# Attention: remainders of the weights of heads 1 to 7 and of the output product by ScalarE and an accumulating transfer

## The chip, the cores and the metric

The kernel runs on one core of a Trainium2 chip. The metric is device time in microseconds (us) of one execution. The core has five instruction streams that run side by side and meet at semaphores: TensorE (PE, the matmuls, with PEld for its weight loads), VectorE (DVE), ScalarE (ACT), GpSimd (POOL) and SyncE (SP). DMA transfers are issued from a queue of SP (the loads of the weights) or of POOL.

## The reference, cut to what matters

The program is a two-layer decoder: one state-space layer with a gated FFN, then one attention layer with a gated FFN, on 512 tokens of width 1024. The change lies in the attention layer, which has 8 heads and a causal mask:

```python
c_q = rms_norm(h @ q_down, q_norm_g)
q = (c_q @ q_up).reshape(b, s, 8, 128 + 64)
k_nope = (c_kv @ kv_up_k).reshape(b, s, 8, 128)
...
scores = (einsum('bqhd,bkhd->bhqk', qn, k_nope)
          + einsum('bqhr,bkr->bhqk', qr, k_rope)) * scale
p = softmax(where(key_idx <= q_idx, scores, -inf))
o = einsum('bhqk,bkhd->bqhd', p, v)
mix = o.reshape(b, s, 1024) @ out_proj
h = layer_norm(DN_ALPHA * h + mix)
```

## The kernel before, in words

**Weights.** Each fp32 product runs as three passes of a rounded format. A weight tile s is split into h, which is s rounded, and the remainder l = s - h; the activations are split alike, and the matmuls compute h·x0 + l·x0 + h·x1 (`mm_a` at lines 159, `mm_b` at lines 165 to 167: h with x0, l with x0, h with x1). `WStream` feeds the weights in a fixed order. `load` issues a tile's transfer on SP into one of six staging buffers `wst` (at most three of them loaded and not yet split), `_split` takes the next tile, writes h into a `wh` buffer on ScalarE (line 96) and l into a `wl` buffer on VectorE (line 97), and lets `fill` issue the next load. There are six `wh` and six `wl` buffers. A buffer can be written again when PE has read the tile that was in it for the last time, so tile i+6 is split only after tile i is done with. `ahead` splits tiles before they are wanted, `get` hands one out, `retire` marks one as read.

**Attention.** `mla_items` lists the tiles: those of the down projections and of v, then `hw[h]` for h = 0 to 7 (128 x 640, the weights of q and k of head h), then `ow[0..7]` (128 x 1024, the rows of the output product that belong to a head). After the down projections, the rotary part `qr` (its last addition is on POOL, line 1119) and v, the program runs a loop over the heads. Iteration h has, in the program's order: `qk(h+1)` and, for even h+1, `qk_rope(h+1)`; the split of one tile; `pv(h-1)`, which sums the head's output in one PSUM bank and splits it into `oT` (ScalarE line 1307, VectorE line 1308); `ptrans(h)`, which transposes the softmax numbers `E` on PE and splits them into `PT` (lines 1290 and 1291); `scores(h+1)`, four query blocks of 128, 256, 384 and 512 keys, with a mask, a maximum, an exponential and a division per block. An iteration with `qk_rope` is called a rope iteration below. The output product comes in two parts: `out_piece(0, 2, i)` uses ow0 and ow1 with heads 0 and 1, `out_piece(2, 6, i)` uses ow2 to ow7. So ow6 and ow7 go into the buffers that ow0 and ow1 leave.

**Order.** The instructions on SP stand in the order of the code. Those of the other engines are put in order by a scheduler when the program is built, so a change in the code can move instructions that it doesn't touch. On the chip each engine takes its instructions strictly in that order.

Of the kernel before, what the change touches and what calls it, by code (L numbers as in the profile page):

```python
# [13 lines left out]
AF = mybir.ActivationFunctionType  # L14
ALU = mybir.AluOpType
# [3 lines left out]
P = 128  # L19
# [9 lines left out]


class WStream:

# [41 lines left out]
    def _split(self, nst=None):  # L76
        nc = self.k.nc
        i = self.split
        f, kind, part = (self.items[i][1:] + (None, None))[:3]
        if kind == "=":  # L80
            self.st[i] = self.st["+"]
        elif i not in self.st:
            self.load(i)
        s = self.st.pop(i)
        if kind == "+":
            self.st["+"] = s
            r = self.sums[part]
            nc.vector.tensor_tensor(r[:, :f], r[:, :f], s[:, :f], op=ALU.add)  # L88
            s = r
        elif kind == "-":  # L90
            nc.vector.tensor_tensor(s[:, :f], self.sums[part][:, :f], s[:, :f], op=ALU.subtract)
        if kind not in ("r", "a", "+"):
            self.out -= 1
        h = self.k.wh.tile([P, 1024], F32R, name="wh")
        l = self.k.wl.tile([P, 1024], F32R, name="wl")
        nc.scalar.copy(h[:, :f], s[:, :f])  # L96
        nc.vector.tensor_tensor(l[:, :f], s[:, :f], h[:, :f], op=ALU.subtract)  # L97
        self.w[i] = (h, l)
        self.split += 1
        self.fill(nst)  # L100
# [956 lines left out]
AH, QR, KVR, RD = 8, 384, 256, 64  # L1057
# [7 lines left out]
def mla_items(dw, vw, rw, hw, ow):  # L1065

    it = [(dw[j], 1024) for j in range(4)] + [(dw[j][:, :768], 768) for j in (4, 5)]
    rv = rw.rearrange("(k p) n -> p k n", p=P)
    it += [(rv[:, 0:2, :], 1024), (rv[:, 2:3, :], 512)]
    vv = vw.rearrange("(k p) n -> p k n", p=P)  # L1070
    it += [(vv[:, :, hf * 512:(hf + 1) * 512], 1024) for hf in range(2)]
    it += [(hw[h], 640) for h in range(AH)]
    it += [(ow[j * P:(j + 1) * P, :], 1024) for j in range(AH)]
    return it


# [318 lines left out]
def trunk_kernel(tc, *aps):  # L1395
    d = dict(zip(_INS, aps))
    out = aps[len(_INS)]
    with ExitStack() as ctx:
        ctx.enter_context(tc.manual_schedule(engines={mybir.EngineType.SP}))
        k = K(tc, ctx)  # L1400
        items = ssd_items(d['xbc'], d['zdt'], d['zw'], d['sow'])
        items += ffn_items(d['up'][0], d['down'][0], RP0)
        items += mla_items(d['dw'], d['vw'], d['rw'], d['hw'], d['aow'])
        items += ffn_items(d['up'][1], d['down'][1], RP1)
        ws = WStream(k, items, k.nb, 3, k.la)
        n = ssd(k, ws, 0, d['xT'], d['x'], d['cw4'], d['hv'], d['sng'], d['gb'][0])
        n = ffn(k, ws, n, d['cw3'][0], d['gb'][1], RP0, la=5, mid=lambda: rope_tables(k, d['pos'], d['freq']))
        n = mla(k, ws, n, d['ang'], d['gb'][2])
        n = ffn(k, ws, n, d['cw3'][1], d['gb'][3], RP1, out=out)
# [53 lines left out]
```

## Time and profile before

| | before |
|---|---|
| median of 3 runs | 1312.31 us (1311.85 to 1312.35) |
| profiled execution | 1311.7 us, of which the span of the profile 1310.0 us |
| PE busy | 1299.5 us, 99% of the span |
| DVE busy | 1020.6 us, 78% |
| ACT busy | 636.0 us, 49% |
| POOL busy | 93.1 us, 7% |
| chain that ended last | PE 95%, DVE 4%, ACT 1% |

The busy times are sums over the span. The chain is followed back from the last instruction, at each step to what released it. The profiled execution is 0.6 us under the median of the runs. TensorE's granted clock was full in the whole span.

### The profile page before, as it was taken

Reading aid. Unit: us, or ns where it says so; the run is one execution under the profiler, and the core shown is the slowest. Engines: PE = TensorE matmul, PEld = TensorE weight load, DVE = VectorE, ACT = ScalarE, POOL = GpSimd, SP = SyncE. Lnnn points to the kernel's source line nnn. Section 1 sums busy time; section 2 is a strip of 40 time slices with the busy share of each in tenths; the row PEclk is TensorE's granted clock in tenths of the full one; section 3 lists DMA queues with packets and bytes.
Section 4 is the critical chain, followed back from the end, with each engine's and each line's share of the span. In section 5 each row is a group of like instructions: output and inputs, shape, how many; then the busy total and the mean of one; then the engine's idle time right before and its main releaser. Section 6 shows DMA issues by size and latency. Waiting matters only on the chain.

```text
span 1310.0 us, 17422 instructions
## 1 busy us (share of the span) xinstructions
PE 1299.5 (99%) x6666; PEld 1098.9 (84%) x6666; DVE 1020.6 (78%) x1581; ACT 636.0 (49%) x1029; POOL 93.1 (7%) x96
## 2 busy tenths in 40 slices
PE   9999999999999999999999999999999999999997
PEld 8888888888888988888888899888898888888886
DVE  7888888797798868866766876898587686667587
ACT  6765555455453544444443434665254444444341
POOL 0111011011011001100000012000100010000000
PEclk9999999999999999999999999999999999999999
DMA  8423322313410433352311822121144227323251
GB/s 297 179 113 129 113 88 90 132 58 133 161 65 10 171 129 81 80 207 98 123 58 31 254 81 62 71 107 49 35 149 135 79 35 213 130 97 105 41 161 65
DMA packets 49779, 144.59 MB, mean 110 GB/s; under 512 B 5312, under 2 KB 6336, under 8 KB 48416
## 3 DMA queue, kind: packets, MB, share of 16 engines
q1 hardware_dynamic: 44480, 133.57, 28.8%
q0 software_dynamic: 5072, 9.77, 4.4%
q8 instruction: 52, 0.85, 0.3%
q14 instruction: 31, 0.25, 0.1%
q10 hardware_dynamic: 144, 0.15, 0.0%
HBM read 141.30 MB, written 2.16 MB: 110 GB/s over the span
## 4 chain that ended last, share of the span: by engine, by line
PE 95%; DVE 4%; ACT 1%; issue 0%; DVEq 0%; ACTq 0%
PE ps L159 57%; PE ps L165 10%; PE ps L167 10%; PE ps L166 10%; PE ps L803 1%; PE ps L915 1%; PE ps L811 1%; PE ps L274 1%; PE ps L792 1%; PE ps L742 1%; PE ps L1265 1%; DVE wl L97 1%; DVE PT L1291 1%; PE ps L770 1%; DVE E L1279 0%; DVE smx L1275 0%
## 5 line engine op out<-in xcount | busy, mean ns | idle before, releaser
L159 PE MATMUL ps<-ht,wh 128*128 128x512 f32 (+1 forms) x2256 | 517.0, 379 | 0.0
L159 PEld LDWEIGHTS ps<-ht,wh 128*128 128x128 f32 x2256 | 408.1, 188 | 79.7 <-issue 1.4
L97 DVE TENSOR_TENSOR wl<-wst,wh 128x1024 fp32r<-128x1024 f32 (+3 forms) x222 | 256.3, 1169 | 44.2 <-ACT wh L96 43.3
L96 ACT CAST wh<-wst 128x1024 fp32r<-128x1024 f32 (+3 forms) x222 | 218.8, 995 | 114.3 <-PE ps L167 62.3
L159 PE MATMUL ps<-ht,wl 128*128 128x512 f32 (+1 forms) x1128 | 266.6, 378 | 0.0
L159 PEld LDWEIGHTS ps<-ht,wl 128*128 128x128 f32 x1128 | 205.2, 188 | 39.6
L328 DVE SCALAR_TENSOR_TENSOR acc<-ps,cw,acc 128x511 f32<-128x511 f32 x88 | 65.7, 747 | 80.0 <-ACT acc L327 80.0
L165 PE MATMUL ps<-wh,gt 128*128 128x512 f32 (+1 forms) x320 | 123.7, 387 | 0.0
L167 PE MATMUL ps<-wh,gt 128*128 128x512 f32 (+1 forms) x320 | 123.6, 386 | 0.0
L166 PE MATMUL ps<-wl,gt 128*128 128x512 f32 (+1 forms) x320 | 123.6, 386 | 0.0
L340 ACT CAST gt<-acc 128x512 fp32r<-128x512 f32 (+1 forms) x80 | 44.0, 571 | 102.0 <-DVE acc L333 99.3
L657 DVE SCALAR_TENSOR_TENSOR cv<-ps,cw,cv 128x511 f32<-128x511 f32 (+2 forms) x96 | 71.3, 746 | 26.8 <-ACT cv L655 25.9
L327 ACT ACTIVATE acc<-ps,cw 128x512 f32<-128x512 f32 x88 | 68.3, 776 | 29.5 <-PE ps L159 29.4
L167 PEld LDWEIGHTS ps<-wh,gt 128*128 128x128 f32 x320 | 60.1, 188 | 12.3
L332 ACT ACTIVATE acc<-acc 128x512 f32<-128x512 f32 x44 | 27.8, 632 | 87.6 <-DVE acc L329 87.5
L165 PEld LDWEIGHTS ps<-wh,gt 128*128 128x128 f32 x320 | 60.1, 188 | 12.1
L166 PEld LDWEIGHTS ps<-wl,gt 128*128 128x128 f32 x320 | 60.1, 188 | 12.1
L329 DVE SCALAR_TENSOR_TENSOR acc<-ps,cw,acc 128x510 f32<-128x510 f32 x88 | 65.8, 748 | 2.5
L52 POOL DMA_DIRECT2D rs<-in_down_dram x24 | 25.4, 1058 | 572.7 <-DVE wl L97 572.7
L96 ACT CAST wh<-rs 128x1024 fp32r<-128x1024 f32 (+1 forms) x48 | 39.9, 834 | 46.4 <-DVE rs L88 27.1
L341 DVE TENSOR_TENSOR gt<-acc,gt 128x512 fp32r<-128x512 f32 (+1 forms) x80 | 48.8, 627 | 13.5 <-ACT gt L340 13.5
L387 DVE SCALAR_TENSOR_TENSOR h<-h,ps 128x512 f32<-128x512 f32 x56 | 37.6, 686 | 26.0 <-PE ps L167 26.0
(242 smaller groups left out, 1744.7 us busy)
## 6 DMA issues: line engine op xcount, KB each, us to landing
wst<-in_up_dram SPq DMA_DIRECT2D x88, 512.0 KB, 3.5
wst<-in_xbc_dram SPq DMA_DIRECT2D x32, 512.0 KB, 6.0
wst<-in_down_dram SPq DMA_DIRECT2D x26, 512.0 KB, 5.5
W<-cumd SPq DMA_DIRECT2D x8, 1024.0 KB, 4.6
wst<-in_sow_dram SPq DMA_DIRECT2D x16, 512.0 KB, 3.6
wst<-in_zw_dram SPq DMA_DIRECT2D x14, 512.0 KB, 6.1
rs<-in_down_dram POOLq DMA_DIRECT2D x12, 512.0 KB, 6.9
wst<-in_down_dram SPq DMA_DIRECT2D x18, 256.0 KB, 2.6
```

Source lines behind the costliest of these rows:

```text
L96: nc.scalar.copy(h[:, :f], s[:, :f])
L97: nc.vector.tensor_tensor(l[:, :f], s[:, :f], h[:, :f], op=ALU.subtract)
L159: nc.tensor.matmul(out, w[:, k, :], xts[k][:, x, ts], start=first and p == 0 and k == 0, stop=last and p == 2 and k == nk - 1, skip_group_ ...
L165: nc.tensor.matmul(out, xt[:, 0, tsl], wh, start=start, stop=False, skip_group_check=True)
L166: nc.tensor.matmul(out, xt[:, 0, tsl], wl, start=False, stop=False, skip_group_check=True)
L167: nc.tensor.matmul(out, xt[:, 1, tsl], wh, start=False, stop=stop, skip_group_check=True)
L327: nc.scalar.activation(a, b, AF.Identity, bias=cw[:, ch, 3:4], scale=cw[:, ch, 2:3])
L328: nc.vector.scalar_tensor_tensor(a[:, 1:], b[:, :SEQ - 1], cw[:, ch, 1:2], a[:, 1:], op0=ALU.mult, op1=ALU.add)
L329: nc.vector.scalar_tensor_tensor(a[:, 2:], b[:, :SEQ - 2], cw[:, ch, 0:1], a[:, 2:], op0=ALU.mult, op1=ALU.add)
L340: k.nc.scalar.copy(dst[:, 0, :], src)
L341: k.nc.vector.tensor_tensor(dst[:, 1, :], src, dst[:, 0, :], op=ALU.subtract)
L657: nc.vector.scalar_tensor_tensor(t[:, d:], b[:, :SEQ - d], cw[:, ch, 3 - d:4 - d], t[:, d:], op0=ALU.mult, op1=ALU.add)
```

## The change

The remainder of 15 of the 16 tiles that the head loop and the output product use, `hw[1]` to `hw[7]` and `ow[0]` to `ow[7]`, is made in another way. They carry the kind "d". ScalarE writes minus the rounded tile into `wl`, and a transfer issued by GpSimd adds the staged tile to it, so that `wl` holds s - h as before. The VectorE subtraction is left out for these tiles. In the changed kernel line 96 is line 97, the new lines are 99 and 100, and lines after `_split` have numbers higher by 5.

```diff
         nc.scalar.copy(h[:, :f], s[:, :f])
-        nc.vector.tensor_tensor(l[:, :f], s[:, :f], h[:, :f], op=ALU.subtract)
+        if kind == "d":
+            nc.scalar.activation(l[:, :f], s[:, :f], AF.Copy, scale=-1.0)
+            nc.gpsimd.dma_start(l[:, :f], s[:, :f], accum_op=ALU.add)
+        else:
+            nc.vector.tensor_tensor(l[:, :f], s[:, :f], h[:, :f], op=ALU.subtract)
...
-    it += [(hw[h], 640) for h in range(AH)]
-    it += [(ow[j * P:(j + 1) * P, :], 1024) for j in range(AH)]
+    it += [(hw[h], 640) + ("d",) * (h > 0) for h in range(AH)]
+    it += [(ow[j * P:(j + 1) * P, :], 1024, "d") for j in range(AH)]
```

On VectorE 15 subtractions go; on ScalarE 15 operations of the same tile sizes come, on GpSimd 15 DMA issues, seven of 128 x 640 and eight of 128 x 1024 fp32. The first place is ScalarE in iteration h=3, a rope iteration, from `qk_rope(4)` to the first `PT`. Before:

```order
L1251 ACTIVATE qrT_7709<-ps 64x512
L1251 ACTIVATE qrT_7712<-ps 64x512
L96 CAST wh<-wst 128x1024
L1307 CAST oT<-ps 128x512
L1290 CAST PT_7742<-ps 128x512
L1290 CAST PT_7749<-ps 128x384
```

And now:

```order
L1256 ACTIVATE qrT_7717<-ps 64x512
L1256 ACTIVATE qrT_7720<-ps 64x512
L97 CAST wh<-wst 128x1024
L99 ACTIVATE wl<-wst 128x1024
L1312 CAST oT<-ps 128x512
L1295 CAST PT_7751<-ps 128x512
```

The new operation stands between the rounding of the weight tile and `oT`, and the same holds in each iteration from h=2 to h=6. The second place is ScalarE at the end of the loop, from the last `PT` of head 7 to the first square sum of the layer norm, where ow6 and ow7 are split. Before:

```order
L1290 CAST PT_8253<-ps 128x256
L1290 CAST PT_8258<-ps 128x128
L96 CAST wh<-wst 128x1024 x2
L1307 CAST oT<-ps 128x512
L194 ACTIVATE lnjunk,lnst<-h,lnst 128x1024
```

And now:

```order
L1295 CAST PT_8271<-ps 128x128
L99 ACTIVATE wl<-wst 128x1024
L97 CAST wh<-wst 128x1024 x2
L99 ACTIVATE wl<-wst 128x1024
L1312 CAST oT<-ps 128x512
L199 ACTIVATE lnjunk,lnst<-h,lnst 128x1024
```

Minus the rounded ow6 now comes first, that of ow7 after both roundings and before `oT`. The third place is PE in `out_piece(2, 6, 0)`, where the first PSUM bank (`ps_8338` before, `ps_8353` now) takes its last three products, those with ow7 (`wh_8332`, `wl_8333` before, `wh_8346`, `wl_8347` now). Before:

```order
L165 MATMUL ps_8338<-wh_8332,oT_8328 128x512
L166 MATMUL ps_8338<-wl_8333,oT_8328 128x512
L167 MATMUL ps_8338<-wh_8332,oT_8328 128x512
L165 MATMUL ps_8339<-wh_7838,oT_7734 128x512
L166 MATMUL ps_8339<-wl_7839,oT_7734 128x512
L167 MATMUL ps_8339<-wh_7838,oT_7734 128x512
```

And now:

```order
L170 MATMUL ps_8353<-wh_8346,oT_8342 128x512
L170 MATMUL ps_8354<-wh_7847,oT_7743 128x512
L171 MATMUL ps_8354<-wl_7848,oT_7743 128x512
L172 MATMUL ps_8354<-wh_7847,oT_7743 128x512
L170 MATMUL ps_8354<-wh_7982,oT_7867 128x512
L171 MATMUL ps_8353<-wl_8347,oT_8342 128x512
L172 MATMUL ps_8353<-wh_8346,oT_8342 128x512
```

Four matmuls of the second bank (`ps_8354`) now stand ahead of the first one that reads the remainder of ow7.

## Rows read from the trace of the kernel before

**Rows 1.** The page: busy us, share of the span, instructions of each engine.

```profile
PE 1299.5 (99%) x6666; PEld 1098.9 (84%) x6666; DVE 1020.6 (78%) x1581; ACT 636.0 (49%) x1029; POOL 93.1 (7%) x96
```

**Rows 2.** Stretches: busy us of each engine, summed over 830 to 920 us.

```profile
sum 90.00, PE 88.12 PEld 76.90 DVE 81.72 ACT 54.79 POOL 0.00; mean PE 9.79 PEld 8.54 DVE 9.08 ACT 6.09 POOL 0.00
```

**Rows 3.** Waits of PE, whole span: engine, line, releaser, us, times, longest.

```profile
PE ps L1288 <- DVE E L1279: 1.0, 2, 0.7
PE ps L1265 <- DVE oT L1308: 0.8, 3, 0.3
PE ps L1265 <- DVE kT L1236: 0.2, 1, 0.2
```

**Rows 4.** Timeline of PE, iteration h=3: start us, us, instruction, idle before.

```profile
869.78 0.34 PE L1265 MATMUL ps<-kb,qrT 128*128 128x384 f32 x1
870.37 0.96 PE L1265 MATMUL ps<-kT,qT 128*128 128x512 f32 x3 [0.25 <-DVE oT L1308]
```

**Rows 5.** Chain of waits, iterations h=1 to h=2: start us, us, what.

```profile
851.14 0.73 DVE wl L97
```

**Rows 6.** Chain of waits, iteration h=3.

```profile
868.37 1.23 DVE wl L97
...
869.62 0.70 DVE oT L1308
```

**Rows 7.** Chain of waits, iteration h=4.

```profile
878.58 0.60 DVE oT L1308
```

**Rows 8.** Chain of waits, iterations h=6 and h=7.

```profile
899.92 0.60 DVE oT L1308
...
902.80 0.47 ACT E L1277 x2
...
907.35 0.88 PE ps L1288 x6
```

**Rows 9.** Timeline of ACT, iterations h=4 and h=6.

```profile
876.27 1.04 ACT L96 CAST wh<-wst 128x1024 fp32r<-128x1024 f32 x1
...
896.48 1.99 ACT L96 CAST wh<-wst 128x1024 fp32r<-128x1024 f32 x2
...
898.84 1.43 ACT L1290 CAST PT<-ps 128x512 fp32r<-128x512 f32 x4
```

**Rows 10.** Groups by form, 780 to 925 us: busy us, mean ns, idle before.

```profile
L97 DVE TENSOR_TENSOR wl<-wst,wh 128x1024 fp32r<-128x1024 f32 x11 | 13.3, 1222 | 0.7 <-ACT wh L96 0.7
L97 DVE TENSOR_TENSOR wl<-wst,wh 128x640 fp32r<-128x640 f32 x8 | 7.6, 956 | 0.0
```

**Rows 11.** Timeline of the tail, PE and ACT.

```profile
915.14 0.39 PE L166 MATMUL ps<-wl,oT 128*128 128x512 f32 x1
...
915.79 2.00 ACT L96 CAST wh<-wst 128x1024 fp32r<-128x1024 f32 x2 [6.60 <-PE ps L167]
...
921.14 0.39 PE L166 MATMUL ps<-wl,oT 128*128 128x512 f32 x1
...
921.82 0.39 PE L166 MATMUL ps<-wl,oT 128*128 128x512 f32 x1
```

**Rows 12.** DMA of 513 to 521 us: issues, KB each, median us to landing.

```profile
rs<-in_down_dram POOLq DMA_DIRECT2D x1, 512.0 KB, 5.6
rs<-in_down_dram POOLq DMA_DIRECT2D x1, 256.0 KB, 4.1
```

**Rows 13.** Line 52, the accumulating loads on POOL, whole span.

```profile
L52 POOL DMA_DIRECT2D rs<-in_down_dram x24: 860/1056/1407, 507.0 to 1258.0; - x24
...
DMA to landing us min/median/max: 4.0/6.7/9.8
```

**Rows 14.** DMA of 780 to 925 us, SP's loads of ow.

```profile
wst<-in_aow_dram SPq DMA_DIRECT2D x8, 512.0 KB, 3.5
```

**Rows 15.** Timeline of POOL and PE ahead of the head loop.

```profile
823.04 1.80 POOL L1119 TENSOR_TENSOR qr<-qr,rtmp 128x512 f32<-128x512 f32 x1 [5.52 <-DVE qr L1118]
...
824.74 0.60 PE L1247 MATMUL ps<-ident,qr 128*128 128x128 f32 x4
```

## The prediction

> **What bounds the kernel now.** The busy shares come first: PE is busy in 99% of the span, VectorE in 78%, ScalarE in 49%, GpSimd in 7% [rows 1]. So VectorE's work is worth something only where PE waits for it. The waits of PE name such places: 2.0 us in all (1.0 + 0.8 + 0.2) in six waits, for the last division of a softmax, for `oT` and for `kT` [rows 3], all of them in the head loop. There VectorE is nearly full, 81.7 of 90 us, while ScalarE has 35 us to spare [rows 2]. A wait row understates the loss, because it is counted from the modelled end of the matmul before. The starts show it: between 869.78 and 870.37 lie 0.59 us [rows 4], where a matmul of 128x384 needs 0.17 (three of 128x512 take 0.68 us from 921.14 to 921.82 [rows 11], 0.23 each, and three quarters of that). The loss is 0.42 and the wait row says 0.25, so I add 0.17 to 0.18 to each of six waits: 2.0 + 6 x 0.18 = 3.1 us. That is all that an unburdened VectorE can give back, 0.24% of the time.
>
> The chain of waits says how those stalls arise. From iteration h=1 to 907.35 us it runs on VectorE and ScalarE alone, and PE only catches up with it; it ends with PE's transposes of head 7 [rows 8]. So what decides there is the length of this chain, from one `oT` to the next, and no sum of busy times.
>
> **What goes and what comes.** VectorE loses eight subtractions of 1.21 us (13.3 / 11) and seven of 0.95 (7.6 / 8) [rows 10], about 16 us. ScalarE gets fifteen operations instead, and I price them as the rounding of the same tile: 2.00 us for two of 128x1024 in a row, 1.99 in another place [rows 9, 11], less the overlap, so 0.95 each. Below that they can hardly come, the shape being the same; a lone one may take 1.04 [rows 9]. GpSimd gets fifteen DMA issues of about 1.1 us each [rows 13], on an engine that does little else. Only the seats on the chain count, so I walk along it.
>
> **The head loop, iteration by iteration.**
> - h=1 to h=2: the subtraction on the chain at 851.14 (0.73 us) goes [rows 5], and the maxima, exponentials and the division for which PE waited up to 0.7 us [rows 3] come that much earlier. ScalarE has its idle gap after `PT` for the new operation. -0.75.
> - h=3 (rope): now the subtraction begins at 868.37, when the weight is rounded, and `oT` at 869.62 [rows 6]. After the change the new operation takes 0.95 on ScalarE from there (869.3), `oT`'s rounding 0.5, a hop 0.05: `oT` on VectorE begins at about 869.87. +0.25. VectorE is free, but it is late because ScalarE now does in a row what the two did side by side.
> - h=4: rounding begins at 876.27 [rows 9], ends 0.95 later, then 0.95 and 0.5: 878.7, against 878.58 [rows 7]. +0.1.
> - h=5 (rope): as h=3. +0.25.
> - h=6: before, two tiles were rounded together from 896.48 [rows 9] and subtracted together, and `oT` began at 899.92 [rows 8]. Now one is split first: 896.48 + 0.95 + 0.95 + 0.5 = 898.9, a gain of 1.0. But then ScalarE does `PT` (1.43 us [rows 9]) and the second tile (1.9) ahead of the exponentials: 898.95 + 1.43 + 1.9 = 902.3, against 902.80 [rows 8]. -0.45, and it lasts to 907.35.
>
> Sum -0.6. The bounds: -3.1, if every stall goes, and +0.6, if only the three losses come. I take -0.6, since it follows the order of the changed ScalarE.
>
> **The tail.** Here ow6 and ow7 are split, into buffers that `out_piece(0, 2, 3)` leaves late, and now a transfer stands between the split and PE. PE reads the remainder of ow0 last at 915.14 + 0.39 [rows 11]. ScalarE writes minus the rounded ow6 from 915.55 to about 916.6 (1.04 for a lone one), and GpSimd issues the transfer. Then come both roundings (1.9, to 918.5) and minus the rounded ow7 (to 919.45), and GpSimd issues at 919.48. PE wants the remainder of ow6 at 921.14. That of ow7 it wanted at 921.82 [rows 11]; the four matmuls that were moved ahead make it 921.82 + 4 x 0.23 = 922.73. With a landing L after the issue the first stall is 916.6 + L - 921.14, and both together are 919.48 + L - 922.73 = L - 3.25, if L is over 3.3. VectorE had both remainders ready at about 919.4, before PE asked, so this is a loss from zero. Nothing hides it: PE has taken all that it could take ahead, and its order is fixed.
>
> L is the uncertain price. No transfer within SBUF stands in the trace. The nearest are the FFN's accumulating loads on the same queue: 5.6 us for 512 KB and 4.1 for 256 KB when little else moves [rows 12], a median of 6.7 and up to 9.8 over all [rows 13]. A plain load of ow on SP, 512 KB in rows of 4096 bytes, takes 3.5 [rows 14]. The new transfer has 512 KB in 128 rows of 4096 bytes, as many rows as the 256 KB one with rows of 2048 bytes, so 4.1 is the bound below. I take 5.6, by the row with the same bytes and the same addition on the way. The tail costs 5.6 - 3.25 = +2.35; with 4.1 it is +0.85, with 6.7 +3.45.
>
> The Trainium skill, page "DMA: Bandwidth & Descriptors", section "Anatomy of one DMA — SWDGE (gpsimd) path", fits such a transfer as 2.0 us plus the bytes over 436 GB/s, which gives an estimate of 3.2 us for 512 KB. The plain load's 3.5 is near it, the accumulating load's 5.6 is not [rows 12, 14], so I let the measurement decide.
>
> **What is hidden.** In h=1 to h=5 the tiles are split some 10 us and more before PE reads them (one tile an iteration, up to six ahead), and their transfers land within that even at 9.8 us. The staging buffer is now freed by the landing, some 6 us later, and SP's loads behind it wait; with six buffers and at most three unsplit, a spare one is there. The FFN's first tiles wait there too, but they are read only after the layer norm. The transfers of heads 1 and 2 stand on GpSimd among the `qr` additions. The last addition ran from 823.04 for 1.80 us, and PE transposes its result at 824.74 [rows 15], a tie. An issue of 1.1 us in front of it begins when ScalarE has written `wl`, near 821.5, and ends about 822.6, so it is hidden by 0.4 us; without that cover it costs up to 0.7.
>
> **Sum.** -0.6 + 2.35 = +1.75 us. The profiled span becomes 1311.75 and its execution, with 1.7 us around the span, 1313.45. The median of the runs lies 0.6 over the profiled execution: 1312.31 + 1.75 = 1314.06, so **1314.1 us**.
>
> **The rivals.**
> - *The transfer of the tail is slow* (slower). The loads of the FFN's weights start just then, and beside other traffic an accumulating transfer took 6.7 us in the median and 9.8 at most [rows 13]. Then the tail costs 3.45 to 6.55 and the time is 1315.2 to 1318.3 us. It decides from L = 6.45 on, where the sum passes 2.6 us, which is 0.2% and about what a measurement can tell from no change. For it: ow6's landing frees a staging buffer and so starts a load that runs beside ow7's transfer. Against it: one load of 512 KB takes 3.5 us and there are at most two. 0.3, and 0.06 more for a chain that loses at every iteration (+0.6) beside an L of 5.6, 1315.3 us.
> - *The transfer is short* (no change). If the new transfer costs no more than a plain load, whose 3.5 us is close to the 3.3 from which a wait begins, the tail loses at most 0.25 us and the head loop's -0.6 stays: 1311.7 to 1312.0 us. For it speaks that the rows are the plain load's 4096 bytes [rows 14], against it every accumulating row. 0.08. The Trainium skill's rule of 3.2 us (the page named above) would end here.
> - *VectorE's relief is the whole story* (faster). The chain of the head loop becomes shorter than PE's work, every stall goes: -3.1. With a tail that costs nothing, 1309.2 us; it decides if the tail costs under 0.5, L under 3.75. For it speaks VectorE's 91% in the loop, against it that `oT` waits for ScalarE, which gets longer. 0.06.
>
> **How the numbers follow.** The forecast has the remaining 0.5, and lies between +0.2 (L of 4.1) and +2.6, so 1312.5 to 1314.9 by itself. Within 0.2% are forecast and short transfer, 0.58; slower 0.36; faster 0.06. The range leaves out the fastest case and the slowest third of the slow transfer: 1311.3 to 1316.8 us.
>
> **What the changed profile would show.** In the waits of PE a new line 171 (the product with l) that waits for a DMA, twice, with some 1.1 and 1.3 us, and the wait for E of up to 0.7 us gone. In the landing times of line 100, medians near 5.6 for 512 KB. `oT` of the rope iterations still on the chain, with ScalarE's line 99 ahead of it in place of VectorE's subtraction. VectorE's busy time lower by about 16 us, and the FFN of the same length. I am wrong if line 99 takes much more than 0.95 us, if PE waits for line 99's `wl` in the loop, or if the transfer slows VectorE or the loads beside it.

## The result, and the profile after

| | before | after |
|---|---|---|
| median of 12 runs each | 1312.28 us (1311.85 to 1312.97) | 1315.41 us (1314.97 to 1315.73) |
| ratio after to before | | 1.0023, interval 1.0015 to 1.0031 |
| profiled execution, its span | 1311.7, 1310.0 us | 1315.5, 1313.5 us |

The change costs 3.1 us (by the interval of the ratio 2.0 to 4.1). The first row of the page shows what was meant to happen to the busy times, against [rows 1]:

```profile
PE 1300.5 (99%) x6666; PEld 1098.5 (84%) x6666; DVE 1005.4 (77%) x1566; ACT 647.7 (49%) x1044; POOL 105.5 (8%) x111
```

VectorE does 15 us less, ScalarE 12 us more, and PE's work is the same. The waits of PE (engine, line, releaser: us, times, longest) are to be held against [rows 3]:

```profile
PE ps L1270 <- DVE oT L1313: 1.8, 2, 1.0
PE ps L171 <- DMA wl<-wst: 1.7, 1, 1.7
...
PE ps L1270 <- DVE kT L1241: 0.2, 1, 0.2
```

The waits for E are too short to be listed now, those for `oT` have doubled, and one for the new transfer is there. The two traces have the same 6666 matmuls, so I compared the start of the same matmul in both (us; the last column is what the stretch since the row above added):

```
place                              before   after   later by   added
second product, early              10.43    10.92    +0.49     +0.49
h=2, first transpose after E      857.29   857.28    -0.01     -0.50
h=3, first matmul after oT        870.37   871.00    +0.63     +0.64
h=4, transpose that needs E       877.25   878.16    +0.91     +0.28
h=5, first matmul after oT        890.58   892.09    +1.51     +0.60
h=6, transpose that needs E       897.45   899.16    +1.71     +0.20
h=6, first matmul after oT        900.58   902.02    +1.44     -0.27
h=7, transpose that needs E       907.35   908.46    +1.11     -0.33
tail, after ow7                   923.18   926.61    +3.43     +2.32
```

The first 0.49 us are no effect of the change: in the thirteen profiles of this study other than that of before this point came 0.0 to 1.2 us later than there, whatever the kernel. Up to the end of the head loop the change loses 0.62 us, in the tail 2.32, 2.94 together. The -0.50 of head 2 is the sum of a new wait for `oT` in h=1, +0.22, and of the wait for E, which is gone, -0.72. Outside these rows the two kernels keep step within 0.15 us, the whole second FFN too.

What happened in a rope iteration, VectorE's timeline shows (h=3; start us, us, instruction, idle before it), to be read beside [rows 6]:

```profile
866.40 0.68 DVE L1257 SCALAR_TENSOR_TENSOR qrT<-ps,qrT 64x512 fp32r<-64x512 f32 x1
867.75 0.69 DVE L1257 SCALAR_TENSOR_TENSOR qrT<-ps,qrT 64x512 fp32r<-64x512 f32 x1 [0.66 <-ACT qrT L1256]
870.25 0.69 DVE L1313 TENSOR_TENSOR oT<-ps,oT 128x512 fp32r<-128x512 f32 x1 [1.81 <-ACT oT L1312]
```

VectorE, freed of the subtraction, stands idle for 1.81 us and waits for ScalarE. ScalarE's timeline has the reason:

```profile
867.12 0.59 ACT L1256 ACTIVATE qrT<-ps 64x512 fp32r<-64x512 f32 x1 [1.12 <-DVE qrT L1257]
867.62 1.03 ACT L97 CAST wh<-wst 128x1024 fp32r<-128x1024 f32 x1
868.55 1.06 ACT L99 ACTIVATE wl<-wst 128x1024 fp32r<-128x1024 f32 x1
869.63 0.59 ACT L1312 CAST oT<-ps 128x512 fp32r<-128x512 f32 x1
```

Rounding and minus the rounded tile stand in a row ahead of `oT`, for which PE waits. In h=2 VectorE waits in the same way, though PE does not (VectorE's timelines, before and now):

```profile
858.28 0.68 DVE L1308 TENSOR_TENSOR oT<-ps,oT 128x512 fp32r<-128x512 f32 x1
```

```profile
858.59 0.69 DVE L1313 TENSOR_TENSOR oT<-ps,oT 128x512 fp32r<-128x512 f32 x1 [1.45 <-ACT oT L1312]
```

In the tail, GpSimd's timeline has the two issues and PE's timeline the two waits, beside [rows 11]:

```profile
917.96 0.86 POOL L100 DMA_DIRECT2D wl<-wst  x1 [12.95 <-ACT wl L99]
920.95 0.86 POOL L100 DMA_DIRECT2D wl<-wst  x1 [2.13 <-ACT wl L99]
```

```profile
921.95 0.39 PE L170 MATMUL ps<-wh,oT 128*128 128x512 f32 x1
922.43 0.50 PE L171 MATMUL ps<-wl,oT 128*128 128x512 f32 x1
...
923.92 0.39 PE L170 MATMUL ps<-wh,oT 128*128 128x512 f32 x1
926.03 0.50 PE L171 MATMUL ps<-wl,oT 128*128 128x512 f32 x1 [1.73 <-DMA wl<-wst]
```

ow6's remainder comes 0.25 us late (0.48 where 0.23 is the pace), ow7's 1.88 (2.11), and a little is lost at the start after each. And the transfers of 919 to 927 us (issues, KB each, median us to landing):

```profile
wst<-in_up_dram SPq DMA_DIRECT2D x2, 512.0 KB, 4.8
wl<-wst POOLq DMA_DIRECT2D x1, 512.0 KB, 5.0
```

### The profile page after: what moved, and what is told of

Same layout as the page of the kernel before. It is cut to its first block, busy times and chain, and to the rows that moved or that the text cites. A ratio compares the mean times of both kernels' runs of the same rounds, so it can differ in the third digit from the quotient of the medians.

```text
span 1313.5 us, 17451 instructions
## 1 busy us (share of the span) xinstructions
PE 1300.5 (99%) x6666; PEld 1098.5 (84%) x6666; DVE 1005.4 (77%) x1566; ACT 647.7 (49%) x1044; POOL 105.5 (8%) x111
## 4 chain that ended last, share of the span: by engine, by line
PE 97%; DVE 1%; DMA 1%; ACT 1%; issue 0%; SPq 0%; DVEq 0%; ACTq 0%
PE ps L164 58%; PE ps L171 10%; PE ps L170 10%; PE ps L172 10%; PE ps L1270 1%; PE ps L808 1%; PE ps L816 1%; PE ps L1307 1%; PE ps L279 1%; PE ps L797 1%; PE ps L747 1%; PE ps L1293 1%; PE ps L920 1%; PE ps L775 1%; DMA xst<-in_xT_dram 0%; DMA wl<-wst 0%
## 5 line engine op out<-in xcount | busy, mean ns | idle before, releaser
L102 DVE TENSOR_TENSOR wl<-wst,wh 128x1024 fp32r<-128x1024 f32 (+3 forms) x207 | 239.9, 1173 | 43.1 <-ACT wh L97 40.6
```

## The experiments

The theory after the result: the change loses at two places, in the head loop because ScalarE makes `oT` later, and in the tail because the last two transfers land late. Each experiment ran against the kernel before on the same chip; its ratio has its interval.

### Which tiles lose: heads only, all but the last two, the last two only

The edits, each to the changed kernel:

```diff
 heads only:
-    it += [(ow[j * P:(j + 1) * P, :], 1024, "d") for j in range(AH)]
+    it += [(ow[j * P:(j + 1) * P, :], 1024) for j in range(AH)]
 last two subtracted (on VectorE, as before):
+    it += [(ow[j * P:(j + 1) * P, :], 1024) + ("d",) * (j < 6) for j in range(AH)]
 last two only:
+    it += [(hw[h], 640) for h in range(AH)]
+    it += [(ow[j * P:(j + 1) * P, :], 1024) + ("d",) * (j >= 6) for j in range(AH)]
```

> Only the weights of heads 1 to 7 take the new way, all eight tiles of the output product are split as before. Theory (the change loses at two places, where ScalarE makes minus the rounded tile of ow ahead of oT, and in the tail where the transfers of ow6 and ow7 land after PE asks): neither place has the new work, so no loss is left, and the wait of PE for E in head 2, 0.7 us and more before, goes: 1311.4 to 1312.3 us, -0.8 to 0 against before. Rival (the transfers or the issues on GpSimd slow the other engines or the loads, or the 0.5 us by which the profiled execution of the changed kernel was later from its 10th microsecond on belongs to the change): 1312.8 us or more, +0.5.

> The changed kernel, but ow6 and ow7 are split on ScalarE and VectorE as before. Theory: the tail's loss goes whole, and the loss of the head loop stays: 1312.6 to 1313.4 us, +0.3 to +1.1 against before; PE waits for no transfer. Rival (the tail's loss is oT of head 7 behind a longer ScalarE, or the transfers crowd the FFN's loads): over 1314.3 us.

> The kernel before, but ow6 and ow7 take the new way. Theory: the tail's loss alone, +2.1 to +2.4 us, 1314.4 to 1314.7 us, with a wait of PE for the transfer of over 1.5 us and landings of 4.5 to 5.1 us; the head loop as before. Rival (the loss comes from the sum of all new transfers): under +1 us, 1313.3 us or less.

Measured: heads only 1311.99 us, ratio 0.9998 (0.9989 to 1.0007); last two subtracted 1312.67 us, 1.0003 (0.9994 to 1.0012); last two only 1314.51 us, 1.0016 (1.0007 to 1.0025). All three lie in the ranges that were forecast for them. So the last two tiles carry 2.1 of the 3.1 us. With heads only, PE's matmuls come 0.50 us earlier from head 2 on, and 0.39 of it is left at the end of the loop; the median's gain of 0.4 us is inside its interval. PE's waits where the last two tiles alone take the new way:

```profile
PE ps L171 <- DMA wl<-wst: 1.4, 2, 1.2
...
PE ps L1293 <- DVE E L1284: 0.9, 2, 0.6
PE ps L1270 <- DVE oT L1313: 0.7, 3, 0.3
```

and where all but they do:

```profile
PE ps L1270 <- DVE oT L1313: 1.8, 2, 0.9
```

The first list is that of before [rows 3] with the transfer added. The second has the two long waits for `oT` and no other one of the loop left. By its trace that kernel loses 0.61 us in the loop; the runs' 0.3 us cannot be told from no change.

### ScalarE's order: the split after oT, with and without the change

```diff
-                with tc.issue_after(a.ins), tc.issue_after(d.ins):
-                    ws.ahead(n[0], most=1)
 ...
-                pv(h - 1)
+                a, d = pv(h - 1)
+            if h + 1 < AH:
+                with tc.issue_after(a.ins), tc.issue_after(d.ins):
+                    ws.ahead(n[0], most=1)
```

(`pv` returns the two instructions that write `oT`.) The same edit was made to the changed kernel, to the kernel before, and to the changed kernel with ow6 and ow7 subtracted on VectorE.

> The changed kernel, but in the loop the split of a weight tile is asked for after oT, so that ScalarE makes oT first and then rounds the tile and writes minus the rounded tile. Theory: the waits of PE for oT in iterations h=3 and h=5 (about 1.1 and 1.0 us) vanish or shrink to under 0.3 each, the tail stays at +2.3: 1312.8 to 1314.0 us. Rival (those waits come from VectorE's queue or from PSUM, not from ScalarE's order): as the changed kernel, 1315.0 us or more.

> The kernel before, but in the loop a weight tile is split after oT. Theory (oT behind the rounding of the weight on ScalarE and behind its subtraction on VectorE makes the waits of PE in h=3, h=5 and h=6): these waits go, 1.2 us in all, and a wait for PT of up to 0.7 us in the rope iterations may take their place as it did with the new way: 1311.4 to 1312.2 us. Rival (VectorE is full, so any order costs the same): 1312.2 to 1312.5 us.

> The changed kernel with both repairs: the split after oT, and ow6 and ow7 subtracted on VectorE as before. Theory (the two losses are separate and add up): the head loop of the run with oT first, -0.7 us, and no loss in the tail: 1311.5 to 1312.0 us, under the kernel before by 0.4 to 0.9. Rival (the losses overlap, so that repairing one uncovers the other): 1312.6 us or more.

Measured: 1314.26 us, ratio 1.0015 (1.0007 to 1.0024); 1312.23 us, 0.9999 (0.9990 to 1.0008); 1311.70 us, 0.9996 (0.9987 to 1.0004). PE's waits in the changed kernel with `oT` first:

```profile
PE ps L171 <- DMA wl<-wst: 1.7, 1, 1.7
...
PE ps L164 <- DVE PT L1296: 1.0, 2, 0.5
PE ps L1293 <- DVE E L1284: 0.4, 1, 0.4
```

The waits for `oT` are gone, so ScalarE's order made them. The two operations now stand ahead of `PT`, and PE waits for that, half as long. By the matmul starts these two cost 0.59 and 0.58 us, and a wait for E in head 7 another 0.48, so the loop wins 0.7 us in all, less than the theory wanted: the time is over its range (1314.0 at most), though under the rival's. The second result lies in the rival's range: in the kernel before, the waits for `oT` went too, but nothing was gained. PE's waits for E there are

```profile
PE ps L1288 <- DVE E L1279: 1.3, 3, 0.6
```

The one in head 2 (0.64) is that of before; those of h=4 (0.32) and h=6 (0.30) are new. In these two iterations ScalarE makes `kT` ahead of the last exponential, as in the changed kernel, and that is a matter of order; that VectorE's load alone makes these waits is not shown. The third result, as forecast, shows that the two losses are separate: without both, the time is 0.6 us under before, which its interval does not tell from no change.

### The landing in the tail: halves, copies, and nothing beside them

```diff
 halves:
-            nc.gpsimd.dma_start(l[:, :f], s[:, :f], accum_op=ALU.add)
+            for c in range(0, f, 512 if f == 1024 else f):
+                e = min(f, c + 512) if f == 1024 else f
+                nc.gpsimd.dma_start(l[:, c:e], s[:, c:e], accum_op=ALU.add)
 plain copy (in the kernel with the last two only):
+            nc.gpsimd.dma_start(l[:, :f], s[:, :f])
 alone (before the splits that release the FFN's loads; with the plain copy, and in the changed kernel):
+                    if stats:
+                        hold = k.small.tile([P, 2], F32, name="hold")
+                        nc.sync.dma_start(hold, k.h[:, 0, :2])
                     ws.ahead(n[0] + nk, 1 if stats else 2)
```

> The changed kernel, but each tile of the output product is added by two transfers of 512 columns instead of one of 1024. PE needs the second half only in the second bank, 18 matmuls later. Theory (PE waits for the landing of the bytes): the first half, 256 KB, lands in about 3.6 us, ow6 in time, ow7 about 1.6 us late: the tail costs 1.6 instead of 2.3, 1314.6 to 1315.0 us. Rival (the fixed part of a transfer makes the wait, its bytes do not matter): first halves land after 4.5 us and more, 1315.4 us or more.

> The kernel before with the new way for ow6 and ow7 only, but the transfer copies the staged tile over minus the rounded tile instead of adding it, so those two remainders hold the whole weight. Same bytes, same rows, same queue. Theory (the addition on the way makes the landing longer, as in the FFN's loads): landing 3.3 to 3.9 us instead of 4.5 to 4.8, the tail's loss 0.5 to 1.2 us instead of 2.0: 1312.9 to 1313.6 us. Rival (bytes and rows make the landing, the addition is free): landing 4.5 us or more, 1314.3 us or more.

> As the run with the plain copy (ow6 and ow7 alone take the new way and their remainders hold the whole weight, since the transfer copies instead of adding), but SP holds the loads of the FFN's weights back until the first rows of the layer norm are written, so that none runs beside the copies. Theory (the second copy took 5.7 us because the first one's landing freed a staging buffer and so started a load beside it): both land in 2.8 to 3.3 us, the tail loses under 0.6 us: 1312.3 to 1313.0 us. Rival (the second transfer of a pair is slow by itself): 5 us and more again, 1315 us or more.

> The changed kernel with the same hold on the loads of the FFN's weights: nothing runs beside the adding transfers of ow6 and ow7. Theory (an adding transfer of 512 KB lands in 4.5 us when alone, 5.0 beside a load): both 4.4 to 4.6 us, the tail loses 1.7 to 1.9 us instead of 2.3: 1314.7 to 1315.0 us. Rival (loads beside it do not matter to an adding transfer): 1315.3 us or more.

Measured: halves 1314.27 us, ratio 1.0015 (1.0006 to 1.0024), under the forecast range, with one wait of PE for a transfer, 1.1 us; plain copy 1316.73 us, 1.0031 (1.0019 to 1.0043); plain copy alone 1312.43 us, 1.0000 (0.9991 to 1.0009); adding alone 1315.16 us, 1.0022 (1.0013 to 1.0031).

The halves came in under the range because the two first halves landed sooner than the 3.6 us that was taken for them, in 3.2 and 3.3. The view of the issue at 918.0 us has the first:

```profile
wl<-wst POOLq DMA_DIRECT2D x1, 256.0 KB, 3.2
```

The plain copy came out in the rival's range, and its five runs spread from 1315.34 to 1317.00. The trace is of the fastest of them; what made the others another 1.4 to 1.7 us slower was not seen. Its landings (line 100):

```profile
DMA to landing us min/median/max: 2.9/4.3/5.7
```

One copy took 2.9 us, the other 5.7. GpSimd's and SP's timelines say what is different for the second:

```profile
917.48 0.63 POOL L100 DMA_DIRECT2D wl<-wst  x1 [92.11 <-ACT wl L99]
920.45 0.53 POOL L100 DMA_DIRECT2D wl<-wst  x1 [2.33 <-ACT wl L99]
```

```profile
920.45 0.33 SPq L55 DMA_DIRECT2D wst<-in_up_dram  x1
920.83 0.43 SPq L434 DMA_DIRECT2D cw<-in_cw_dram  x1
```

The first copy landed at 920.4 and freed its staging buffer, SP issued the next load of FFN weights into it at 920.45, and at the same moment the second copy was issued. With that load held back, both landings are short (the same view of that run):

```profile
DMA to landing us min/median/max: 2.9/2.9/3.0
```

PE's waits name no transfer there, and by the matmul starts the tail loses 0.2 us. So the second copy was slow by what its twin released, not by itself. The two adding transfers, when alone, land in 4.5 us (DMA of 914 to 930 us):

```profile
wl<-wst POOLq DMA_DIRECT2D x2, 512.0 KB, 4.5
```

and in the changed kernel the second one, partly beside a load, in 5.0. By its trace the hold brings the tail from 2.3 to 1.85 us, as forecast; the median, 1315.16, lies between the theory's range and the rival's, 0.25 under the changed kernel, which is inside the interval. Adding costs 1.6 us on top of a copy (4.5 against 2.9). That a copy wins so much from the hold and the adding transfer so little is what the landings show; why is open. The two cases are not alike: beside the copy the load began together with it, in the changed kernel at 922.43, 1.5 us after the issue.

### Where the two operations fit: the split after PT

```diff
-                a, d = qk_rope(h + 1) or ends
-                with tc.issue_after(a.ins), tc.issue_after(d.ins):
-                    ws.ahead(n[0], most=1)
+                qk_rope(h + 1)
```

The split that is asked for after `ptrans` stays, so an iteration now asks for one tile instead of two, and tiles of the output product are left for the end of the loop. This was made in the changed kernel with ow6 and ow7 subtracted on VectorE, and in the kernel before.

> The changed kernel with ow6 and ow7 subtracted on VectorE, and with the split of a weight tile asked for only after PT, in ScalarE's pause before the exponentials (1.7 to 2.0 us in iterations h=2 and h=3). Theory (the loss of the head loop is the place of the two ScalarE operations ahead of oT or of PT): the waits for oT and for PT go, those for E stay under 0.5 us each: 1310.6 to 1311.5 us, 0.8 to 1.7 under the kernel before. Rival (the pause is too short, the exponentials come late and PE waits for E instead): 1311.7 us or more.

> The kernel before, all subtractions on VectorE, with the split asked for only after PT as in the fastest run. Theory (both are needed: the place frees ScalarE's way to oT and PT, and VectorE without the subtractions has the time to use it; with the subtractions VectorE stays full and PE waits for E, as in the run of the kernel before with oT first): 1311.3 to 1312.6 us, within 0.1% of before. Rival (the place alone does it): 1309.3 to 1310.3 us.

Measured: the first 1309.41 us, ratio 0.9978 (0.9970 to 0.9987), faster than both kernels and than forecast; the second 1311.33 us, 0.9992 (0.9983 to 1.0001). Of PE's waits in the head loop the first has only this one left:

```profile
PE ps L1270 <- DVE kT L1241: 0.2, 1, 0.2
```

ScalarE in its h=3 shows why (timeline; compare 869.63 for `oT` above):

```profile
865.96 0.59 ACT L1256 ACTIVATE qrT<-ps 64x512 fp32r<-64x512 f32 x1 [1.00 <-DVE qrT L1257]
866.58 0.59 ACT L1312 CAST oT<-ps 128x512 fp32r<-128x512 f32 x1
867.06 1.42 ACT L1295 CAST PT<-ps 128x512 fp32r<-128x512 f32 x4
868.33 0.77 ACT L97 CAST wh<-wst 128x640 fp32r<-128x640 f32 x1
868.96 0.78 ACT L99 ACTIVATE wl<-wst 128x640 fp32r<-128x640 f32 x1
870.28 0.37 ACT L1282 ACTIVATE E<-ps,smx 128x128 f32<-128x128 f32 x1 [0.55 <-DVE smx L1280]
```

The two operations fill a pause in which ScalarE waited for VectorE's maxima anyway, and 0.55 us of it is left. In the kernel before the same place gains about 0.9 us and leaves these waits of PE:

```profile
PE ps L1288 <- DVE E L1279: 1.2, 2, 0.9
```

Both stand in head 7, 0.24 us and this one:

```profile
907.31 0.66 PE L1288 MATMUL ps<-ident,E 128*128 128x128 f32 x4 [0.94 <-DVE E L1279]
```

VectorE's timeline shows what stands among the last divisions of head 7. ScalarE had just rounded four tiles of the output product in a row (from 898.15, 3.92 us), and VectorE subtracts two of them ahead of the division that PE waits for:

```profile
904.12 1.21 DVE L97 TENSOR_TENSOR wl<-wst,wh 128x1024 fp32r<-128x1024 f32 x1
905.24 0.42 DVE L1279 TENSOR_SCALAR E<-E,smx 128x384 f32<-128x384 f32 x1
905.57 0.16 DVE L1278 RECIPROCAL smx<-smx 128x1 f32<-128x1 f32 x1
905.64 1.21 DVE L97 TENSOR_TENSOR wl<-wst,wh 128x1024 fp32r<-128x1024 f32 x1
906.76 0.49 DVE L1279 TENSOR_SCALAR E<-E,smx 128x512 f32<-128x512 f32 x1
```

Up to `oT` of h=6 the place alone wins as much as both together, 2.2 us against 2.3 by the matmul starts; the waits for E in head 2 and for `oT` are gone with every subtraction still on VectorE. In head 7 the kernel with both wins another 0.6, while the place alone loses 1.0. Busy times of 830 to 920 us, the fastest kernel first, then the kernel before with the same place (compare [rows 2]):

```profile
sum 90.00, PE 89.85 PEld 79.56 DVE 72.50 ACT 63.18 POOL 8.59; mean PE 9.98 PEld 8.84 DVE 8.06 ACT 7.02 POOL 0.95
```

```profile
sum 90.00, PE 88.67 PEld 78.11 DVE 82.42 ACT 55.73 POOL 0.00; mean PE 9.85 PEld 8.68 DVE 9.16 ACT 6.19 POOL 0.00
```

By the medians the place alone wins 0.9 us, the new way alone (without ow6 and ow7) loses 0.3, and both together win 2.9. The place alone came out at the lower edge of what the theory expected, and its interval just takes in no change. So both were needed for the whole gain here. The reason in the theory, a VectorE that stays full over the loop, is not what the traces show: VectorE is as busy as before, and apart from 0.2 us for `kT` PE waits for it in head 7 alone. Whether the place with another order of the subtractions in head 7 would win the whole 2.9 us was not tried.

## Why the prediction was right, and where it was not

The direction, the range and the size of the tail held; 1314.1 us was forecast and 1315.41 measured, and the missing 1.3 us lie in the head loop (1.2 of them by the traces).

- **What there was to win.** 3.1 us of stalls, worked out from wait rows and starts. The fastest run took out 2.9 us by its trace and by its median, and left one stall (for `kT`). The size held. That it is an unburdened VectorE that gives it back did not: in the kernel before the place of the split alone took out 2.2 us of it up to h=6, with VectorE as full as ever.
- **The head loop, -0.6 forecast, +0.6 measured.** The step that failed is the first one of the walk, -0.75 for h=1 to h=2. It puts the new operation into ScalarE's gap after `PT` and goes on to h=3. But in h=1 and h=2, as later, ScalarE rounds a tile and writes minus the rounded tile ahead of `oT`. In h=1 that cost PE 0.22, and PE's gain after E was 0.50. In h=2 PE does not wait for `oT`, so its starts don't show the loss there, but VectorE's timeline does. With the 0.49 us of the traces' start taken off, VectorE's `oT` of h=2 came only 0.18 us earlier than before (at +0.31, where PE's transposes are at -0.01). With heads only, where that row of ScalarE is as before, it came 0.47 earlier (start taken off too).
- **From h=3 on.** The chain keeps the +0.31 up to the rounding of h=3 (867.62 against 867.30), and there the longer row adds as much again: 0.93 + 1.08 + 0.62 = 2.63 us to VectorE's `oT` (starts 867.62, 868.55, 869.63, 870.25) against 2.32 (867.30 and 869.62), near the +0.25 that I had. The two make the +0.64 of PE in h=3. h=5 repeats it: VectorE's `oT` stands at +1.10 in h=4 and at +1.42 in h=5. That a gain is carried on along the chain, as the sum takes for granted, held where ScalarE has no longer row from h=2 on: with heads only, 0.39 of the 0.50 us are still there in head 7. The run with `oT` first shows that the row makes the two waits, since both are gone there.
- **The chain of the loop.** It does not run on VectorE and ScalarE alone, as I had read it. After the stall of h=3 it stands on PE for 3.5 us, up to the product for q, for which ScalarE's `qT` waits, so what PE loses in h=3 goes on into h=4 (chain of waits before: start us, us, what):

```profile
870.37 1.42 PE ps L1265 x5
871.79 2.07 PE ps L159 x9
```

- **h=4, +0.1 forecast, +0.28 measured, and h=6, +0.20 at E.** The scheduler also put `kT` ahead of the last exponential in these two iterations (in h=4 `kT` at 875.92, the exponential at 876.42; before, at 875.79 and 875.12), and PE waits for E. The order of the changed kernel has it, and the walk did not take it in. The gain in h=6 came as forecast, -0.40 in sum for -0.45.
- **The tail, +2.35 forecast, +2.32 measured.** The mechanism is right, and the fit is partly luck: the landing was 4.4 us for ow6 and 5.0 for ow7 and not 5.6, but GpSimd began each issue 0.3 to 0.45 us after ScalarE's end and not 0.03, and ScalarE's operations took 1.05. The two stalls were 0.25 and 1.88 us, not 1.1 and 1.3. ow6's landing, with no load beside it, was nearer to the accumulating load with as many rows, 4.1 us for 256 KB in 128 rows [rows 12], than to the one with as many bytes, 5.6, which the sum took.
- **The slow transfer as a rival.** Its mechanism, a load that the first landing starts, is real: it costs the adding transfer about 0.5 us (4.5 to 5.0) and a copy 2.8 (2.9 to 5.7). It was too small here to decide. The range that was to leave out the slowest third of this rival ends at 1316.8 us, near the middle of its 1315.2 to 1318.3.
- **The short transfer as a rival.** A copy lands in 2.9 us when alone, an adding transfer in 4.5. The estimate of 3.2 us by the Trainium skill's fit ("DMA: Bandwidth & Descriptors", "Anatomy of one DMA — SWDGE (gpsimd) path") is near the copy's 2.9, and not near the addition's 4.5; no number of this study rests on it.
- **What I had called hidden.** The `qr` addition, the early heads and the FFN lose nothing: the offset of the two traces is steady up to h=1 and after the tail. That a spare staging buffer is there was wrong: SP's loads did wait for the landings of ow6 and ow7. They were early enough, and this is what sends a load beside ow7's transfer.

## What to carry to other kernels

When work is moved from a full engine to an idle one, look at what stands behind it in the idle engine's queue: the rounding and the new operation cost 0.6 us ahead of `oT`, and in a pause that ScalarE had anyway, a few rows later, PE waited for neither. Where a chain runs over two engines that worked side by side, moving one part makes the sum of both the length, in every iteration where the part stands on the chain, also in one where the bounding engine does not wait. A high busy share does not say that an engine is what PE waits for: here a change of order alone took out the stalls up to head 7 and left VectorE as full as it was. A transfer in place of an instruction needs its landing time as a lead, so leave out the tiles that are wanted at once.

## What the runs showed of the hardware that was not expected

- A copy of 512 KB within SBUF on GpSimd's queue landed in 2.9 us and its adding twin in 4.5 us, both alone. Beside a load of 512 KB the copy took 5.7 us.
- The issue of an adding transfer of 512 KB took GpSimd 0.86 us in the changed kernel, that of a copy 0.53 to 0.63.
- The start of the program varies: the first product's matmuls came 0.0 to 1.2 us later from one profiled execution to another. Differences of two profiles are better read from matmul to matmul than from the spans.
